# Rotary embedding of split heads: VectorE's program placed at a block of 128 instructions, with landings awaited by other engines

## The chip, the core and the metric

The kernel runs on one core of a Trainium2 chip. The metric is the device time of one execution in microseconds, lower is better. Five engines with instruction streams of their own take part: TensorE (PE), VectorE (DVE), ScalarE (ACT), GpSimd (POOL) and SyncE (SP); 16 DMA engines move data between HBM and the on-chip memory.

## What is computed

`x` has 16 x 512 rows of 1024 floats: 16 heads of 64, each in two halves of 32. `cos` and `sin` have one row of 32 floats for each of the 512 positions. Cut to what matters:

```python
x = x.reshape(batch, seq, num_heads, head_dim)
x1, x2 = x[..., :half_dim], x[..., half_dim:]
rotated = concatenate([x1 * cos - x2 * sin, x1 * sin + x2 * cos], axis=-1)
```

That is 33.55 MB in and 33.55 MB out, in fp32.

## The kernel before

The 8192 rows are cut into 8 tiles of 1024 rows. In a tile each of the 128 partitions holds 8 rows that follow each other in HBM. One such row on all partitions (128 x 1024 floats) is a **unit**; there are 64, and `u` counts them. The tiles lie in a ring of 40 places in `x_sb`, so tiles 5, 6 and 7 reuse the places of tiles 0, 1 and 2 (tile 7 those from 16 on), and a result overwrites its input there.

Each unit takes three steps:

- the **cosine product** x * cos, written to one of three PSUM buffers `t1_ps`: always VectorE, line 347;
- the **sine product** of the swapped halves with (-sin, sin), written to one of six buffers `t2_sb`: GpSimd for most (line 305 two units at once, line 166 one), VectorE for nine (line 166);
- the **sum**: VectorE for 45 units (`comb`, line 356, back into `x_sb`); for the other 19 (`PE2`) TensorE adds `t2_sb` into `t1_ps` through an identity matrix (line 265), and ScalarE copies the result to `x_sb` (line 227).

The order on VectorE is written out: the cosine product of unit `u`, then the sum of unit `u - 1` where that is VectorE's. A cosine product waits until the buffer of unit `u - 3` is free: for a `PE2` unit by ScalarE's semaphore `act`, else by its own semaphore `comb`.

DMA. Nine loads are issued from ScalarE's queue (line 189, q10 in the profile): loads 0 and 1 are the halves of tile 0 (2 MB each), loads 2 to 8 are tiles 1 to 7 (4 MB each). Loads 0 to 5 are issued at once. Loads 6, 7 and 8 (`late`, tiles 5 to 7) are issued in ScalarE's loop behind units 21, 28 and 37, once the stores of the places that they overwrite have landed. The two tables come on the same queue behind load 0 (line 211). Ten stores are issued from SyncE's queue (line 202, q1): two halves of tile 0, tiles 1 to 6, two halves of tile 7. A store waits for the sums of its units, from ScalarE and from VectorE.

Start. VectorE clears a small tile (line 315); TensorE multiplies it six times into `t1_ps` to set PSUM's accumulate bits (line 238, semaphore `sem_w`), and then, once the tables have landed, spreads them into PSUM (line 248). ScalarE makes the sine table from that (lines 222 and 223).

Waits for landings. `wait_landed` waits for `sem_in` of a load at the load's first unit. Before the change GpSimd calls it for each unit (line 291 on) and VectorE does too, in `mul` (line 332). An instruction that needs several semaphores gets a separate semaphore instruction ahead of it, so VectorE's program has 132 instructions: 118 tensor-tensor operations, ten semaphore instructions, one each of drain, memset, scalar product and copy.

Of the kernel before, what the change touches and what calls it, by code (L numbers as in the profile page):

```python
# [6 lines left out]
def bass_split_heads_rope_kernel(  # L7
# [38 lines left out]
    first_row = [sum(t[0] for t in TILES[:i]) for i in range(len(TILES))]  # L46
    NU = sum(t[0] for t in TILES)
    assert NU * P == batch * seq
    NT = len(TILES)
# [3 lines left out]
    loads = []  # L53
# [14 lines left out]
    PE2 = [u in (5, 7) or R1 * 2 <= u < NU - 3 * R1 and u % 8 in (1, 3, 5) for u in range(NU)]  # L68
# [7 lines left out]
    SHARED = 3  # L76
# [4 lines left out]
    NT1 = 3  # L81
    NT2 = 6
    BANK = 512
    EH = H * HD // BANK
    LEAD = 1


    alone = [(not V2[u] or u == SHARED) and not (u and TWO[u - 1]) for u in range(NU)]
# [2 lines left out]
    with ExitStack() as stack:  # L91
# [13 lines left out]
        sem_in = [stack.enter_context(nc.semaphore(f"in{i}")) for i in range(len(loads))]  # L105
# [8 lines left out]
        sem_w = stack.enter_context(nc.semaphore("bits"))  # L114
# [72 lines left out]
        def load(eng, i):  # L187
            t, o, m = loads[i]
            eng.dma_start(in_sbuf(t, o, m), in_dram(xf, t, o, m)).then_inc(sem_in[i], 16)  # L189

        def wait_landed(eng, t, r):
            if (t, r) in load_at:
                eng.wait_ge(sem_in[load_at[t, r]], 16)
# [11 lines left out]
        def on_scalar(ae):  # L205
            early = [i for i in range(len(loads)) if i not in late]
            for i in early:
                load(ae, i)
                if i == 0:
                    for c, (table, sem) in enumerate(((cos, sem_cos), (sin, sem_sin))):  # L210
                        ae.dma_start(stage[:, c, :], table.rearrange("(s r) d -> s (r d)", r=R1)).then_inc(sem, 16)  # L211
            ae.wait_ge(sem_i, 2)
            for n in SIZES:
                m = n // R1
                ae.activation(  # L215
                    pick[n][:],
                    ident[:].rearrange("q (s k) -> q k s", k=m)[:, :, None, :].broadcast_to([P, m, m, P // m]),
                    COPY,
                ).then_inc(sem_g, 1)
            for i, n in enumerate(SIZES):  # L220
                ae.wait_ge(sem_t, i + 1)
                ae.activation(s_sb[n][:, :, 0, :], raw_sin[n], COPY, scale=-1.0)  # L222
                ae.activation(s_sb[n][:, :, 1, :], raw_sin[n], COPY).then_inc(sem_s, 1)  # L223
            for u in range(NU):
                if PE2[u]:
                    ae.wait_ge(sem_e, n_pe[u])
                    ae.activation(xs[:, place_of(u), :], t1_ps[:, u % NT1, :], COPY).then_inc(sem_a, 1)  # L227
                for i in late:
                    if BEHIND[i] == u:
                        for j in TILES[loads[i][0]][4]:  # L230
                            ae.wait_ge(sem_out[j], 16)
                        load(ae, i)

        def on_tensor(pe):
            pe.wait_ge(sem_z, 1)
            for k in range(NT1):
                for b in range(EH):
                    pe.matmul(  # L238
                        t1_ps[:, k, b * BANK:(b + 1) * BANK], zero[:, 0:P], zero[:], start=True, stop=True
                    ).then_inc(sem_w, 1)  # L240
            pe.wait_ge(sem_g, len(SIZES))
            pe.wait_ge(sem_cos, 16)
            pe.wait_ge(sem_sin, 16)
            pe.wait_ge(sem_w, NT1 * EH)
            for n in SIZES:
                for c, to in enumerate((c_ps[n], raw_sin[n])):
                    for k in range(n // R1):
                        ins = pe.matmul(  # L248
                            to[:, k * R1:(k + 1) * R1, :].rearrange("p r d -> p (r d)"),
                            pick[n][:, k].rearrange("q b s -> q (b s)"),  # L250
                            stage[:, c, :],
                            start=c == 0,
                            stop=True,
                            skip_group_check=c == 1,
                        )
                ins.then_inc(sem_t, 1)
            for u in range(NU):
                if not PE2[u]:
                    continue
                if TWO[u - 1]:  # L260
                    pe.wait_ge(sem_q[(u - 1) % NT2], made[u - 1])
                pe.wait_ge(sem_q[u % NT2], made[u])
                t2 = t2_sb[:, u % NT2, :, :, :].rearrange("p h t d -> p (h t d)")
                for b in range(EH):
                    ins = pe.matmul(  # L265
                        t1_ps[:, u % NT1, b * BANK:(b + 1) * BANK],
                        ident[:],
                        t2[:, b * BANK:(b + 1) * BANK],
                        start=False,
                        stop=True,  # L270
                        skip_group_check=True,
                    )
                ins.then_inc(sem_e, 1)

        def on_gpsimd(pl):
            pl.memset(ident[:], 1.0).then_inc(sem_i, 1)  # L276
            pl.wait_ge(sem_i, 1)
            pl.affine_select(  # L278
                out=ident[:],
                in_=ident[:],  # L280
                compare_op=mybir.AluOpType.is_equal,
                fill=0.0,
                base=0,
                pattern=[[-1, P]],
                channel_multiplier=1,
            ).then_inc(sem_i, 1)
            seen = set()
            for u in range(NU):
                t, r = rows[u]
                n = TILES[t][0]  # L290
                wait_landed(pl, t, r)
                if V2[u] and u != SHARED or (u and TWO[u - 1]):
                    continue
                if n not in seen:
                    seen.add(n)
                    pl.wait_ge(sem_s, SIZES.index(n) + 1)
                m = 2 if TWO[u] else 1
                for v in range(u, u + m):
                    if v == u + m - 1 or PE2[v - NT2] != PE2[v + 1 - NT2]:
                        wait_t2_free(pl, v)  # L300
                k = place_of(u)
                if m == 1:
                    heads(pl, u, 0, CUT if u == SHARED else H, s_sb[n][:, r]).then_inc(sem_q[u % NT2], 1)
                else:
                    pl.tensor_tensor(  # L305
                        t2_sb[:, u % NT2:u % NT2 + 2].rearrange("p n h t d -> p (n h) t d"),
                        x_sb[:, k:k + 2, :, ::-1, :].rearrange("p n h t d -> p (n h) t d"),
                        s_sb[n][:, r:r + 2].rearrange("p n t d -> p n (t d)")[:, :, None, :].broadcast_to(
                            [P, 2, H, HD]
                        ),  # L310
                        mult,
                    ).then_inc(sem_q[u % NT2], 1)

        def on_vector(ve):
            ve.memset(zero[:], 0.0).then_inc(sem_z, 1)  # L315
            ve.wait_ge(sem_w, NT1 * EH)
            seen = set()

            def own_sines():
# [8 lines left out]
            def mul(u):  # L328
                t, r = rows[u]
                n = TILES[t][0]  # L330
                k = place_of(u)
                wait_landed(ve, t, r)
                if n not in seen:
                    seen.add(n)
                    ve.wait_ge(sem_t, SIZES.index(n) + 1)
                if u == NT1 - 1:
                    own_sines()
                if V2[u]:
                    wait_t2_free(ve, u)
                    heads(ve, u, CUT if u == SHARED else 0, H, v_ps[n][:, V_ROWS[n].index(r)])  # L340
                if u >= NT1:
                    v = u - NT1
                    if PE2[v]:
                        ve.wait_ge(sem_a, n_pe[v])
                    else:
                        ve.wait_ge(sem_v, n_comb[v])
                ve.tensor_tensor(  # L347
                    t1_ps[:, u % NT1, :].rearrange("p (h d) -> p h d", d=HALF),
                    x_sb[:, k, :, :, :].rearrange("p h t d -> p (h t) d"),
                    c_ps[n][:, r, :][:, None, :].broadcast_to([P, 2 * H, HALF]),  # L350
                    mult,
                ).then_inc(sem_q[u % NT2], 1)
# [9 lines left out]

            for u in range(NU + LEAD):

                ahead = u == SHARED + LEAD
                if ahead:
                    comb(u - LEAD)
                if u < NU:
                    mul(u)
                if u >= LEAD and not ahead and not PE2[u - LEAD]:  # L370
                    comb(u - LEAD)

# [38 lines left out]
```

## Time and profile before

| what | value |
|---|---|
| median of 3 runs | 161.0 us (161.0 to 161.33) |
| the profiled execution | 161.04 us, span 159.8 us |
| VectorE busy | 134.1 us, 84% of the span, 121 instructions |
| GpSimd busy | 126.5 us, 79%, 40 instructions |
| TensorE, ScalarE busy | 56.3 us (35%), 21.8 us (14%) |
| HBM read, written | 33.69 MB, 33.55 MB: 421 GB/s over the span |
| one product or sum on VectorE (128 x 1024) | 1.22 us |
| one double sine product on GpSimd (128 x 2048) | 4.52 us |
| one copy on ScalarE | 1.02 us |

How to read it: the span runs from the first to the last instruction of the profiled execution, and the execution's time has some 1.2 us around it. The page's slices show busy tenths in 40 equal parts of the span. The row DMA is the mean busy share of the 16 DMA engines, and the queue rows give the packets of each queue, their bytes and the time that they took as a share of 16 engines' span. A view of a window counts the packets that start in it. The timeline gives start, length, engine, line, operation, and in brackets the idle time before and what ended it. In the waits, "A <- B" is A's idle time that B ended.

### The profile page before, as it was taken

How to read it: one execution, taken by the hardware profiler on the slowest of the kernel's cores; microseconds unless marked ns; L12 is line 12 of the kernel's file. 1: busy time of each engine (PE TensorE's matmuls, PEld its weight loads, DVE VectorE, ACT ScalarE, POOL GpSimd, SP SyncE). 2: the span in 40 equal slices, each digit the busy share in tenths (PEclk: the TensorE clock that was granted, in tenths of full speed). 3: DMA queues.
4: the chain of work that ended last, by engine and by line, in shares of the span. 5: the costliest groups of instructions: out<-in, count | busy, mean ns of one | idle time of the engine just before them, and what ended most of it. 6: DMA issues, size and time to landing. Idle time of an engine off the chain costs nothing.

```text
span 159.8 us, 449 instructions
## 1 busy us (share of the span) xinstructions
PE 56.3 (35%) x90; PEld 19.6 (12%) x90; DVE 134.1 (84%) x121; ACT 21.8 (14%) x23; POOL 126.5 (79%) x40
## 2 busy tenths in 40 slices
PE   6050007744407740788066407740575000000000
PEld 1040002111102110222021102110220000000000
DVE  0028997999999999998999999999799987999500
ACT  0410000331300330022203300330022000000000
POOL 1009999999999999999999999956999289990000
PEclk9999999999985899557659985899557655555555
DMA  5999998999999999999999999999999999999996
GB/s 172 418 426 459 435 476 336 422 414 418 500 406 455 435 427 394 420 492 402 394 500 410 402 484 427 402 427 484 402 394 509 402 402 476 435 402 443 406 439 287
DMA packets 3025, 67.25 MB, mean 421 GB/s; under 512 B 336, under 2 KB 592, under 8 KB 592
## 3 DMA queue, kind: packets, MB, share of 16 engines
q10 hardware_dynamic: 1584, 33.69, 49.8%
q1 hardware_dynamic: 1440, 33.56, 48.8%
q14 instruction: 1, 0.01, 0.0%
HBM read 33.69 MB, written 33.55 MB: 421 GB/s over the span
## 4 chain that ended last, share of the span: by engine, by line
DMA 45%; DVE 34%; POOL 11%; PE 1%; issue 1%; ACTq 1%; ACT 0%; SPq 0%; POOLq 0%
DMA x_sb<-in_x_dram 21%; DMA out_dram<-x_sb 20%; DVE t_ps L347 18%; DVE x_sb L356 14%; POOL t_sb L305 6%; POOL t_sb L166 5%; DMA stage<-in_sin_dram 4%; DVE t_sb L166 3%; PE tab_ps L248 1%; PE t_ps L248 1%; ACTq L211 0%; ACT sine L222 0%; ACTq L189 0%; ACT sine L223 0%; SPq L177 0%
## 5 line engine op out<-in xcount | busy, mean ns | idle before, releaser
L305 POOL TENSOR_TENSOR t_sb<-x_sb,sine 128x2048 f32<-128x2048 f32 x22 | 99.0, 4524 | 6.6 <-DMA x_sb<-in_x_dram 6.6
L347 DVE TENSOR_TENSOR t_ps<-x_sb,tab_ps 128x1024 f32<-128x1024 f32 x64 | 76.8, 1221 | 11.3 <-PE t_ps L248 9.9
L265 PE MATMUL t_ps<-t_sb,ident 128*128 128x512 f32 x76 | 51.5, 818 | 59.4 <-DVE t_ps L347 38.6
L356 DVE TENSOR_TENSOR x_sb<-t_ps,t_sb 128x1024 f32<-128x1024 f32 x45 | 54.7, 1219 | 3.7 <-POOL t_sb L305 3.0
L166 POOL TENSOR_TENSOR t_sb<-x_sb,sine 128x1024 f32<-128x1024 f32 (+1 forms) x12 | 27.6, 2307 | 10.4 <-ACT sine L223 10.4
L227 ACT ACTIVATE x_sb<-t_ps 128x1024 f32<-128x1024 f32 x19 | 19.4, 1023 | 91.9 <-PE t_ps L265 89.9
L265 PEld LDWEIGHTS t_ps<-t_sb,ident 128*128 128x128 f32 x76 | 17.1, 250 | 92.7 <-issue 53.6
L166 DVE TENSOR_TENSOR t_sb<-x_sb,tab_ps 128x1024 f32<-128x1024 f32 (+1 forms) x9 | 10.1, 1124 | 0.0
L238 PE MATMUL t_ps<-zero 128*128 128x512 bf16 x6 | 2.7, 630 | 1.3 <-DVE zero L315 1.3
L248 PE MATMUL tab_ps<-stage,chosen 128*128 128x128 f32 x4 | 1.2, 454 | 4.9 <-DMA stage<-in_sin_dram 4.9
L215 ACT ACT_TABLE_LOAD x1 | 1.3, 1283 | 4.8 <-issue 4.8
L248 PEld LDWEIGHTS tab_ps<-stage,chosen 128*128 128x128 f32 x4 | 0.9, 322 | 5.8 <-issue 5.8
L248 PE MATMUL t_ps<-stage,chosen 128*128 128x128 f32 x4 | 1.1, 421 | 0.0
L315 DVE MEMSET zero<- 128x256 uint32 x1 | 0.3, 272 | 0.9 <-PEq L393 0.9
L238 PEld LDWEIGHTS t_ps<-zero 128*128 128x128 bf16 x6 | 0.7, 137 | 2.4 <-DVE zero L315 1.2
L222 ACT ACTIVATE sine<-t_ps 128x256 f32<-128x256 f32 x1 | 0.4, 383 | 4.4 <-PE t_ps L248 4.4
L248 PEld LDWEIGHTS t_ps<-stage,chosen 128*128 128x128 f32 x4 | 1.0, 333 | 0.0
L276 POOL MEMSET ident<- 128x128 f32 x1 | 0.2, 204 | 0.3 <-POOLq L393 0.3
L215 ACT ACTIVATE chosen<-ident 128x256 f32<-128x256 f32 x1 | 0.4, 429 | 0.0
L223 ACT ACTIVATE sine<-t_ps 128x256 f32<-128x256 f32 x1 | 0.4, 378 | 0.0
L278 POOL TENSOR_SCALAR_AFFINE_SELECT ident<-ident 128x128 f32<-128x128 f32 x1 | 0.3, 292 | 0.1
L393 POOL MEMSET const-float32-0.0<- 128x1 f32 x1 | 0.1, 98 | 0.3 <-issue 0.3
(5 smaller groups left out, 0.7 us busy)
## 6 DMA issues: line engine op xcount, KB each, us to landing
x_sb<-in_x_dram ACTq DMA_DIRECT2D x7, 4096.0 KB, 33.2
out_dram<-x_sb SPq DMA_DIRECT2D x6, 4096.0 KB, 30.2
out_dram<-x_sb SPq DMA_DIRECT2D x4, 2048.0 KB, 16.4
x_sb<-in_x_dram ACTq DMA_DIRECT2D x2, 2048.0 KB, 9.4
stage<-in_cos_dram ACTq DMA_DIRECT2D x1, 64.0 KB, 7.2
stage<-in_sin_dram ACTq DMA_DIRECT2D x1, 64.0 KB, 7.0
```

The lines of the kernel that those rows point to most:

```text
L166: return eng.tensor_tensor(t2_sb[:, u % NT2, a:b, :, :], swapped(place_of(u))[:, a:b], table[:, None, :, :].broadcast_to([P, b - a, 2, HALF]),
L215: ae.activation(pick[n][:], ident[:].rearrange("q (s k) -> q k s", k=m)[:, :, None, :].broadcast_to([P, m, m, P // m]), COPY,).then_inc(se ...
L222: ae.activation(s_sb[n][:, :, 0, :], raw_sin[n], COPY, scale=-1.0)
L223: ae.activation(s_sb[n][:, :, 1, :], raw_sin[n], COPY).then_inc(sem_s, 1)
L227: ae.activation(xs[:, place_of(u), :], t1_ps[:, u % NT1, :], COPY).then_inc(sem_a, 1)
L238: pe.matmul(t1_ps[:, k, b * BANK:(b + 1) * BANK], zero[:, 0:P], zero[:], start=True, stop=True).then_inc(sem_w, 1)
L248: ins = pe.matmul(to[:, k * R1:(k + 1) * R1, :].rearrange("p r d -> p (r d)"), pick[n][:, k].rearrange("q b s -> q (b s)"), stage[:, c, :] ...
L265: ins = pe.matmul(t1_ps[:, u % NT1, b * BANK:(b + 1) * BANK], ident[:], t2[:, b * BANK:(b + 1) * BANK], start=False, stop=True, skip_group ...
L278: pl.affine_select(out=ident[:], in_=ident[:], compare_op=mybir.AluOpType.is_equal, fill=0.0, base=0, pattern=[[-1, P]], channel_multiplier=1,
L305: pl.tensor_tensor(t2_sb[:, u % NT2:u % NT2 + 2].rearrange("p n h t d -> p (n h) t d"), x_sb[:, k:k + 2, :, ::-1, :].rearrange("p n h t d ...
L347: ve.tensor_tensor(t1_ps[:, u % NT1, :].rearrange("p (h d) -> p h d", d=HALF), x_sb[:, k, :, :, :].rearrange("p h t d -> p (h t) d"), c_ps ...
L356: ve.tensor_tensor(xs[:, place_of(u), :], t1_ps[:, u % NT1, :], t2_sb[:, u % NT2, :, :, :].rearrange("p h t d -> p (h t d)"), add,).then_i ...
```

## The change

Four edits move VectorE's waits for landings to other engines, and one places its program.

- VectorE's wait for the six zero products (`sem_w`) goes; TensorE itself waits for them before the tables, as before.
- VectorE waits for a landing only in the last tile (`in8`). For the rest:
  - TensorE waits for load 0 before it spreads the tables, which VectorE waits for;
  - GpSimd waits for load 1 before the sine product of unit 3 (`SHARED`), whose sum comes before VectorE's first product of load 1;
  - ScalarE waits for the load of tiles 1 to 6 before its copy of the unit three ahead of the tile's first (units 5, 13, 21, 29, 37 and 45, the `carrier`s), since VectorE's first product of the tile waits for that copy.
- `addr_align(128, offset=0, max_nops=0)` behind VectorE's memset asks the loader to put the next instruction at a multiple of 128 places in VectorE's stream; the padding is jumped over.

VectorE's program has 125 instructions afterwards, the directive among them, and 121 behind the directive. The order of the arithmetic and of the DMAs on each engine is unchanged; ScalarE has six more semaphore instructions.

```diff
+    BLOCK = 128
...
+        carrier = {}
+        for i, (t, o, _) in enumerate(loads):
+            if t == 0:
+                assert o in (0, SHARED + 1)
+            elif t < NT - 1:
+                assert PE2[first_row[t] - NT1]
+                carrier[first_row[t] - NT1] = i
...
                 if PE2[u]:
+                    if u in carrier:
+                        ae.wait_ge(sem_in[carrier[u]], 16)
                     ae.wait_ge(sem_e, n_pe[u])
...
             pe.wait_ge(sem_w, NT1 * EH)
+            pe.wait_ge(sem_in[0], 16)
...
                 wait_landed(pl, t, r)
+                if u == SHARED:
+                    wait_landed(pl, t, r + 1)
...
             ve.memset(zero[:], 0.0).then_inc(sem_z, 1)
-            ve.wait_ge(sem_w, NT1 * EH)
+
+            ve.addr_align(BLOCK, offset=0, max_nops=0)
...
-                wait_landed(ve, t, r)
+                if t == NT - 1:
+                    wait_landed(ve, t, r)
```

## Prediction

> **What bounds the kernel.** I read the page's slices and its DMA queues first, since VectorE is 84% busy but the busiest row of all is the DMA's:
>
> ```profile
> DMA  5999998999999999999999999999999999999996
> ...
> q10 hardware_dynamic: 1584, 33.69, 49.8%
> q1 hardware_dynamic: 1440, 33.56, 48.8%
> q14 instruction: 1, 0.01, 0.0%
> ```
>
> Loads (q10) and stores (q1) take 49.8% + 48.8% = 98.6% of what 16 DMA engines have in the span; only the first and the last slice are open. The packet records behind this row agree: 1,664 packets of 32 KB at 1.213 us and 768 of 16 KB at 0.611 us are 2,487 us, or 155.5 us on each of 16 engines, and each engine starts between 1.82 and 2.87 us and is then never free until it ends. So a shorter wait on VectorE moves nothing as long as the DMA queues hold work, and the time is that of the DMA engine that ends last.
>
> The third queue is the one that the change is about: one packet of instructions inside the span. A window of 10 ns finds it, and the timeline of VectorE shows what ran:
>
> ```profile
> DMA packets 1, 0.01 MB, mean 819 GB/s; under 512 B 0, under 2 KB 0, under 8 KB 0
> ...
> q14 instruction: 1, 0.01, 193.1%
> ```
>
> ```profile
> 63.49 1.22 DVE L347 TENSOR_TENSOR t_ps<-x_sb,tab_ps 128x1024 f32<-128x1024 f32 x1
> 64.62 1.22 DVE L356 TENSOR_TENSOR x_sb<-t_ps,t_sb 128x1024 f32<-128x1024 f32 x1
> 65.75 1.22 DVE L347 TENSOR_TENSOR t_ps<-x_sb,tab_ps 128x1024 f32<-128x1024 f32 x1
> 66.88 1.21 DVE L166 TENSOR_TENSOR t_sb<-x_sb,tab_ps 128x1024 f32<-128x1024 f32 x1
> ```
>
> The packet starts at 65.52 us, has 8,192 bytes and takes 0.309 us. VectorE starts an instruction every 1.13 us straight across it: the fetch did not hold VectorE. Whose fetch is it? If a packet is a block of 128 instructions, as the change takes it, VectorE's 132 can't lie in one block and must enter another once; the span has one such packet, and VectorE runs about its 56th instruction. The other candidate is PE, with 90 weight loads and 90 matmuls in the trace, which started again at 64.86 us after 6 us of idle time. I take it to be VectorE's, by the count, and keep PE for a rival.
>
> What the fetch does hold is the DMA engine that carried it. In the packet records that engine's next packet (32 KB, at 65.82) takes 1.564 us for 1.213; with the fetch it lost 0.309 + 0.351 = 0.66 us. Every transfer closes with a 4-byte packet on each of the 16 engines (under 512 B in the rows). Load 5 closes first 15 times by 69.38 us, then once at 69.81; the final store closes 15 times by 159.03 and once at 159.41. Three windows, 69.4 to 69.9, 158.6 to 159.03 and 159.03 to 159.8:
>
> ```profile
> DMA packets 3, 0.07 MB, mean 131 GB/s; under 512 B 1, under 2 KB 1, under 8 KB 1
> ```
> ```profile
> DMA packets 16, 0.02 MB, mean 38 GB/s; under 512 B 15, under 2 KB 15, under 8 KB 15
> ```
> ```profile
> DMA packets 1, 0.00 MB, mean 0 GB/s; under 512 B 1, under 2 KB 1, under 8 KB 1
> ```
>
> The reader is to see one straggler, alone, from the fetch to the end of the span. Packet by packet, end to start, the chain from the fetch leads to load 5's straggler. At load 4's close, before the fetch, the last two engines are 0.04 us apart (51.19 and 51.23), not 0.43.
>
> **The change part by part.** All sums are against the profiled execution, 161.04 us with its span of 159.8 (1.24 lie around it); the median of the runs is 161.0, so I forecast on 161.04 and compare with 161.0.
>
> 1. *The alignment.* The directive becomes padding that is jumped over once, behind the memset at 0.92 us. VectorE then waits for the tables until 11.09 (9.9 us idle, released by PE L248), which hides a jump of any price below that. Behind it stand 121 instructions, so 7 places of 128 are left and the program crosses no block between 11 and 150 us. The fetch at 65.5 goes. Without its 0.66 us the straggler would end at 158.75, and the 15 others set the end. What is late next is the second engine: 0.38 us earlier by packets (159.41 to 159.03), or 0.27 us by the semaphore's steps (159.76 to 159.49), since landings are reported at different delays. The gain is 0.27 to 0.38.
>
> [...] No row shows a fetch during the start. Bounds: 0 (before the first load packet at 1.82) and 0.66 us of straggling as at 65.5. I take 0 to 0.3: engines whose first packets come 1.05 us apart (1.82 to 2.87) close load 0 within 0.46 us (7.75 to 8.21 by the semaphore's steps), so a late starter catches up more than half. That leaves at most 158.75 + 0.3 = 159.05, level with the second engine, and costs nothing.
>
> [...]
>
> 2. *VectorE's waits.* Of ten semaphore instructions eight go, with the waits for eight landings and for the zeros of PE. They last 0.02 to 0.05 us and lie beside the running operation (starts stay 1.13 us apart across them): worth 0. PE's added wait for load 0 (landed 8.21 us) stands before the wait for the tables' data (8.65): 0. GpSimd's added wait for load 1 (landed 13.49) stands before its fourth product, at about 18 us: 0.
>
> 3. *ScalarE's six added waits.* Behind each stands a copy (L227) and whatever VectorE and the stores wait for of it. Landings against the copy's start: load 2 at 23.2 against 28.9, load 3 at 37.0 against 43.1, load 4 at 51.6 against 58.9, load 5 at 70.3 against 76.2, load 6 at 89.6 against 91.1: five come earlier and cost 0. Load 7 comes at 109.00, its copy was at 106.94:
>
> ```profile
> 106.94 1.02 ACT L227 ACTIVATE x_sb<-t_ps 128x1024 f32<-128x1024 f32 x1 [2.43 <-PE t_ps L265]
> 109.24 1.22 DVE L347 TENSOR_TENSOR t_ps<-x_sb,tab_ps 128x1024 f32<-128x1024 f32 x1
> 111.66 0.33 SPq L202 DMA_DIRECT2D out_dram<-x_sb  x1
> 113.61 1.23 DVE L356 TENSOR_TENSOR x_sb<-t_ps,t_sb 128x1024 f32<-128x1024 f32 x1 [0.89 <-POOL t_sb L305]
> ```
>
> That copy moves to about 109.0 and ends at 110.0; VectorE's product at 109.24 needs it and moves to about 110.1, 0.85 late. Two more operations follow, then the 0.89 us in which VectorE waits for GpSimd takes it up: back in step at 113.6. The store at 111.66 leaves at about 112.5; the store before it lands at 130.8, so the queue is covered for 18 us. Load 8 was issued earlier, at 95.2. Cost 0.
>
> Sum: 161.04 − 0.27 to 0.38 = 160.66 to 160.77. I forecast **160.7 us**.
>
> **Rivals.**
>
> *Nothing gained, 161.0.* The fetch stays under the loads or stores once and the straggler remains: because the jump's fetch costs its whole 0.66 at the start, because seven instructions beyond the last one enter the next block at 150 us, because the fetch was PE's, or because the padding is not placed as the directive asks (the change would then not do what it says). Against: the count above, and the catching up in the first 6 us. For: PE's start at 64.86, 0.66 us ahead of the packet, and no row tells what VectorE executes after 150 us.
>
> [...]
>
> *Two fetches instead of one, slower: 161.3 to 161.7.* The block is entered at 1 us, and, since only 7 places are left behind the 121, the next one at about 150 us, when VectorE is done and stores still run until 159.4. Should both fall on the same DMA engine under traffic, it loses 1.32 us for 0.66: at most 161.04 + 0.66 = 161.70; with half of the first caught up 161.04 + 0.3 = 161.34. It decides only if VectorE passes those 7 places before 159 us.
>
> *ScalarE's late copy starves the stores, 161.2 to 161.9.* VectorE's 0.85 us at 109 would have to reach the end, in part or whole (161.04 + 0.85 = 161.89). The last store is issued at 150.09, and the one ahead of it closes at 154.55, so 4.4 us are covered; for a loss of even 0.2 us the delay must grow past 4.6. I see no such growth.
>
> **How the numbers follow.** Forecast 0.60, no gain 0.25, two fetches 0.10, late copy 0.05. A measurement of this kernel tells about 0.2%, 0.32 us, from no change. The forecast's gain lies just around that: 0.27 and 0.38 on one side and the other, up to 0.66 if the straggler also held back others. Of its 0.60 I put 0.41 beyond 0.2% and 0.19 within. Faster 0.41; within 0.19 + 0.25 = 0.44; slower 0.10 + 0.05 = 0.15. The range: 161.04 − 0.66 = 160.4 below; above, no gain with the spread of the runs (161.33) and the cheap end of the two fetches (161.34): 161.4. It leaves out some 0.15.
>
> **What would show it.** Right: queue q14 has no packet between 5 and 159 us, at most one near 1 to 3; the last window holds no lone 4-byte packet 0.4 us behind the rest; 14 of 16 engines close load 5 within about 0.3 us (two come earlier, as before); VectorE's row at 109 is about 0.85 late, and in step again at 113.6. Wrong: a q14 packet at 150 us or midway, a straggler with no fetch in the span, or a DMA slice below 9 between the first and the last.

## The result, and the profile after

The changed kernel takes 162.39 us (median of 6 runs, 161.93 to 162.54) for 161.0 before: a ratio of 1.0079, with a 95% interval of 1.0068 to 1.009. It is slower by 0.8%; the forecast was 160.7, in a range of 160.4 to 161.4.

The profiled execution takes 161.93 us with a span of 160.07; before it was 161.04 with 159.79. So of 0.89 us more in the profiles, 0.28 lie in the span and 0.61 around it (1.86 for 1.25). Over all six runs the time around the span is 1.83 to 2.04, and the span 160.0 to 160.5, in four of them 160.5.

The page's DMA rows, for those of before: full to the same extent, and again one packet of instructions in the span.

```profile
DMA  5999998999999999999999999999999999999896
...
q10 hardware_dynamic: 1584, 33.69, 49.7%
q1 hardware_dynamic: 1440, 33.56, 48.7%
q14 instruction: 1, 0.01, 0.0%
```

But the packet has moved. The window from 4.68 to 4.70 us holds it, and the one from 161.5 to 162.5 us, behind the span, a second one:

```profile
DMA packets 1, 0.01 MB, mean 410 GB/s; under 512 B 0, under 2 KB 0, under 8 KB 0
...
q14 instruction: 1, 0.01, 98.8%
```
```profile
DMA packets 1, 0.01 MB, mean 8 GB/s; under 512 B 0, under 2 KB 0, under 8 KB 0
...
q14 instruction: 1, 0.01, 2.1%
```

The straggler is there from the start. Load 0 lands on 15 DMA engines by 8.15 us and on the last at 9.12 (before: 8.18 and 8.21). The window from 8.3 to 9.3 us has three late closing packets, the last ones of load 0 and of the two tables; before (the first line) it has none:

```profile
DMA packets 27, 0.44 MB, mean 442 GB/s; under 512 B 0, under 2 KB 0, under 8 KB 0
```
```profile
DMA packets 48, 0.48 MB, mean 483 GB/s; under 512 B 3, under 2 KB 19, under 8 KB 19
```

At the end the windows 158.5 to 159.2 and 159.2 to 159.8 us show it as before, 15 closing packets and then a single one; the packet records put them at 159.07 and 159.70 (before 159.03 and 159.41):

```profile
DMA packets 16, 0.02 MB, mean 23 GB/s; under 512 B 15, under 2 KB 15, under 8 KB 15
```
```profile
DMA packets 1, 0.00 MB, mean 0 GB/s; under 512 B 1, under 2 KB 1, under 8 KB 1
```

The timeline around 109 us shows ScalarE's copy waiting for load 7, as the prediction had it, and VectorE back near its old place (113.98 for 113.61):

```profile
109.19 1.02 ACT L241 ACTIVATE x_sb<-t_ps 128x1024 f32<-128x1024 f32 x1 [3.33 <-DMA x_sb<-in_x_dram]
109.46 1.21 DVE L375 TENSOR_TENSOR x_sb<-t_ps,t_sb 128x1024 f32<-128x1024 f32 x1
110.59 1.22 DVE L366 TENSOR_TENSOR t_ps<-x_sb,tab_ps 128x1024 f32<-128x1024 f32 x1
...
113.01 0.33 SPq L214 DMA_DIRECT2D out_dram<-x_sb  x1
113.98 1.21 DVE L375 TENSOR_TENSOR x_sb<-t_ps,t_sb 128x1024 f32<-128x1024 f32 x1
```

### The profile page after: what moved, and what is told of

It reads as the page before. It is cut to its first block, busy times and chain, and to the rows that moved or that the text cites. A ratio compares the mean times of both kernels' runs of the same rounds, so it can differ in the third digit from the quotient of the medians.

```text
span 160.1 us, 448 instructions
## 1 busy us (share of the span) xinstructions
PE 56.6 (35%) x90; PEld 19.9 (12%) x90; DVE 134.0 (84%) x121; ACT 21.8 (14%) x23; POOL 126.5 (79%) x40
## 4 chain that ended last, share of the span: by engine, by line
DMA 45%; DVE 35%; POOL 11%; PE 1%; ACTq 1%; ACT 0%; issue 0%; SPq 0%; POOLq 0%
DMA x_sb<-in_x_dram 21%; DMA out_dram<-x_sb 19%; DVE t_ps L366 18%; DVE x_sb L375 14%; POOL t_sb L322 6%; POOL t_sb L167 5%; DMA stage<-in_sin_dram 5%; DVE t_sb L167 3%; PE tab_ps L263 1%; PE t_ps L263 1%; ACTq L223 0%; ACT sine L234 0%; ACTq L190 0%; ACT sine L235 0%; SPq L178 0%
```

## The experiments

Two theories stood against each other. **Placement**: the fetch at 4.69 us makes a worse straggler than the one at 65.5, and VectorE's end, 7 places ahead of a block's end, costs time behind the span. **Waits**: the moved waits cost the time. Each diff is against the changed kernel unless it says otherwise. "Lag" is the last DMA engine's closing packet of the final store less the last but one, in the profiled execution (a second late engine makes it small: in e1 the last three close at 159.03, 159.30 and 159.43); "around" is the time less the span, over all runs of the kernel. "Left" is the number of places from the program's end to the next multiple of 128, as the directive sets it.

| kernel | left | fetches, us | lag, us | profiled span, us | around, us | median, us | ratio to before (95%) |
|---|---|---|---|---|---|---|---|
| before | | 65.52 | 0.38 | 159.8 | 1.2 to 1.3 | 161.0 | |
| changed | 7 | 4.69, 161.89 | 0.63 | 160.1 | 1.83 to 2.04 | 162.39 | 1.0079 (1.0068 to 1.009) |
| e1 waits only | | 64.32 | 0.13 | 159.8 | 1.19 to 1.29 | 161.1 | 1.0005 (0.9996 to 1.0014) |
| e2 align only | 127 | 3.77, 133.95 | 2.31 | 161.7 | 1.21 to 1.28 | 162.37 | 1.009 (1.0069 to 1.0112) |
| e3 offset 64 | 71 | 4.58, 68.92 | 1.63 | 161.0 | 1.20 to 1.30 | 161.88 | 1.0051 (1.0032 to 1.0071) |
| e4 offset 112 | 23 | 5.68 | 1.34 | 160.8 | 1.19 to 1.27 | 161.7 | 1.0045 (1.0031 to 1.006) |
| e5 offset 7 | 0 | 4.45, 133.36 | 1.69 | 161.1 | 1.19 to 1.28 | 162.31 | 1.0068 (1.0049 to 1.0087) |
| e6 offset 124 | 11 | 5.74 | 0.95 | 160.4 | 1.20 to 1.29 | 161.77 | 1.0039 (1.0025 to 1.0054) |
| e7 offset 98 | 37 | 30.16 | 0.14 | 159.6 | 1.19 to 1.29 | 160.89 | 0.9988 (0.9978 to 0.9998) |
| e8 padding run through | 7 | 7.46, 161.95 | 0.78 | 160.2 | 1.79 to 1.96 | 162.28 | 1.0066 (1.0048 to 1.0085) |
| e9 offset 127 | 8 | 5.25, 162.29 | 0.98 | 160.5 | 2.04 | 162.34 | 1.0083 (1.0064 to 1.0102) |
| e10 offset 4 | 3 | 4.66, 161.82 | 0.80 | 160.5 | 1.36 to 1.58 | 162.01 | 1.006 (1.0037 to 1.0083) |
| e11 offset 104 | 31 | 20.10 | 0.62 | 160.4 | 1.20 to 1.28 | 161.41 | 1.0025 (1.0015 to 1.0035) |
| e12 offset 98 again | 37 | 30.46 | 0.49 | 159.9 | 1.20 to 1.29 | 160.92 | 0.9997 (0.9988 to 1.0006) |

**The halves apart: e1 and e2.** e1 leaves the directive out:

```diff
-            ve.addr_align(BLOCK, offset=0, max_nops=0)
```

> The changed kernel without the alignment directive: VectorE's waits are moved, its program lies where it lay. Two theories. Placement: the loss of the changed kernel comes from the placement alone, in two pieces. The fetch at 4.69 us makes one DMA engine close everything 0.6 to 1.0 us after the others (span 160.07 for 159.79 in the profiles, 160.5 in most timed runs), and VectorE's program, ending 7 places before a block's end, crosses into the next block after the span (161.93 - 160.07 = 1.86 us around the span for 161.04 - 159.79 = 1.25). Then this kernel takes 161.0 us, with 1.2 to 1.3 us around the span, no fetch before 60 us and one at 65 to 73 us (eight semaphore instructions less, so the block's end falls some five operations of 1.13 us later). Waits: the loss comes from the moved waits (tables 0.8 us later, ScalarE's copy held for load 7). Then it takes 162.2 to 162.5 us. If the fetch stays at 65.5 us, it is not VectorE's place that sets it.

161.1 us, the same as before, and 1.2 us around the span. The moved waits cost nothing that can be measured: the theory of the waits falls. One detail was expected wrongly: the fetch came at 64.32 us and not some five operations later. VectorE had 75 instructions left there, the running one among them, and 76 in the kernel before. Eight instructions fewer moved the block's end with the program's end, as if a program without the directive were laid by its end.

e2 is the kernel before with the directive alone:

```diff
             ve.memset(zero[:], 0.0).then_inc(sem_z, 1)
+            ve.addr_align(128, offset=0, max_nops=0)
```

> The kernel before with the alignment directive behind VectorE's memset and nothing else: 129 instructions stand behind the directive, one more than 128. Placement: one fetch at about 4.7 us as in the changed kernel and a second one when the last instruction is reached, at 147 to 151 us, under the stores. The straggler then loses some 0.66 us more: span 160.7 to 161.2; the program ends one place into a fresh block, so 1.2 to 1.3 us around the span; in all 162.0 to 162.4. Waits: no wait is moved, so 161.0 us.

162.37 us, from the directive alone: placement. Both fetches are there and the time around the span is 1.21 to 1.28, but the second came at 133.95 us, when VectorE was 15 instructions ahead of the multiple, and not at 147 to 151. The straggler closed 2.31 us behind the others, more than the two fetches account for: it was 0.96 us behind at load 0 and 1.70 at load 8, still ahead of the second fetch. That the time is so near the changed kernel's 162.39 is chance, since all of e2's loss lies in the span and half of the changed kernel's around it.

**Other places in the block: e3 and e4.** One number is changed:

```diff
-            ve.addr_align(BLOCK, offset=0, max_nops=0)
+            ve.addr_align(BLOCK, offset=64, max_nops=0)   # e4: offset=112
```

> The changed kernel with the program placed 64 places behind a multiple of 128. It enters a block by the jump and crosses the next multiple after 64 instructions, and ends 57 places into that block, with 71 left. Placement: two fetches, at about 4.7 us and at 70 to 80 us, both under traffic; span 160.7 to 161.2 us; 1.2 to 1.3 us around the span since no end of a block is near; in all 162.0 to 162.4. If instead the jump itself costs the time around the span, 1.86 us stay around it and the whole is 162.6 to 163.0. Waits: 162.2 to 162.5 with nothing changed against the changed kernel.

> The changed kernel with the program placed 112 places behind a multiple of 128. The program before crossed its block's end at about its 54th instruction, so it lies some 76 places into a block at the directive; place 112 is then in the same block, and no block is entered at the start. [...] Placement: no fetch at 4.7 us, one at 20 to 26 us; load 0 closes on all engines by 8.3 us; the straggler loses 0.66 us or less, since packets are slow from 24 to 35 us anyway (0.65 us a DMA engine in the profile of before), so the span is 159.4 to 159.8; the crossing behind the span stays, 1.86 us around it; in all 161.3 to 161.7. If the jump costs the time around the span and not the crossing: 161.3 to 161.7 too, but then offset 64 keeps 1.86. Waits: 162.2 to 162.5.

e3 had its two fetches (4.58 and 68.92 us) and 1.25 us around the span, so the jump by itself does not cost the time there; 161.88 us is a little less than expected. e4 gave 161.7 us as a number, but neither way of getting it held: the fetch was at the start (5.68 us) although no block should have been entered, and the time around was 1.19 to 1.27 us, not 1.86. That 23 places left cost time behind the span was an estimate: no row shows how many instructions VectorE runs there. No other fetch follows in e4. The window 5.67 to 5.70 us has the fetch, and in the packet records the engine's next packet, 16 KB, takes 1.147 us for 0.611: with the fetch 0.85 us lost. (The changed kernel's fetch lost about as much: 0.316 us, and 1.134 for 0.611 in the packet behind it.) At the end (159.1 to 160.7 us) one engine still moves two data packets when the rest has closed:

```profile
DMA packets 2, 0.02 MB, mean 819 GB/s; under 512 B 0, under 2 KB 0, under 8 KB 0
...
q10 hardware_dynamic: 1, 0.02, 127.3%
q14 instruction: 1, 0.01, 64.4%
```
```profile
DMA packets 3, 0.03 MB, mean 20 GB/s; under 512 B 1, under 2 KB 1, under 8 KB 1
```

So 161.7 - 161.0 = 0.7 us of the loss belong to a fetch at the start and what becomes of it (the engine was 0.76 us behind at load 0 and 1.34 at the end), and the rest of the changed kernel's 1.39 us, 0.7, is what it has more around the span. The changed kernel's own runs divide the same way: the median span is 160.5 us, for 159.7 in the runs of before beside e1, and some 1.9 us lie around it for 1.24.

**What costs behind the span: e5, e6, e8, e9, e10.** e5 is `offset=7`, e6 `offset=124`, e9 `offset=127`, e10 `offset=4`; e8 runs through the padding:

```diff
-            ve.addr_align(BLOCK, offset=0, max_nops=0)
+            ve.addr_align(BLOCK, offset=0, max_nops=255)
```

> The changed kernel with the program 7 places behind a multiple of 128, so that its last instruction is the last place of its block. In the runs so far a fetch came when VectorE was 14 to 15 instructions ahead of a multiple (offset 64: the 50th behind the directive; alignment alone: the 113th), and only the changed kernel, which ends 7 places ahead of one, has 1.83 to 2.04 us around the span; all others have 1.2 to 1.3. If what follows the kernel pays for the crossing, this kernel, where nothing but what follows lies behind the multiple, shows whether it is the crossing itself or the few places left: with 1.2 to 1.3 around the span the few places are what costs, with 1.8 to 2.0 any end up to the multiple does. If the fetch comes 14 to 15 instructions ahead whatever the program does, there are two: at 4 to 6 us and at about 141 us, and the span is 161.0 to 161.7, in all 162.2 to 163. If there is no second fetch, the span is 160.0 to 160.5 and the whole 161.3 to 162.5.

> The changed kernel with the program 124 places behind a multiple of 128: it crosses after 4 instructions and ends 11 places ahead of the next multiple. If few places left behind the program cost the time around the span, by the distance of 14 to 15 instructions seen at the other fetches, 1.8 to 2.0 us stand around the span (23 left at offset 112: 1.2 to 1.3). If it is the placement at a multiple itself, 1.2 to 1.3. One fetch at 4 to 6 us, the straggler as at offset 112, span 160.2 to 160.8. In all 162.0 to 162.8 by the first, 161.4 to 162.1 by the second.

> The changed kernel with max_nops=255: VectorE runs through the padding instead of jumping over it; the program lies at the same multiple of 128 and ends 7 places ahead of the next. If the jump makes the fetch late and dear, the fetch comes earlier or as it came before, close to the first packets at 1.8 to 3 us, and the straggler loses less: span 159.5 to 159.8. If only the place counts, the fetch stays at 4 to 6 us with a span of 160.0 to 160.5. Around the span 1.8 to 2.0 us in both, since the end lies where it lay; with 1.2 to 1.3 there the jump would be the cause.

> The changed kernel with the program 127 places behind a multiple of 128: it ends 8 places ahead of one (the changed kernel: 7, with 1.79 to 2.04 us around the span whether the padding is jumped over or run through; offset 124: 11, with 1.20 to 1.29). If the places left at the end decide, the turn lies between 7 and 11 and this run places it: 1.8 to 2.0 or 1.2 to 1.3. If it is the program's first place, exactly a multiple, that costs, 1.2 to 1.3 here and in the next run. One fetch at 4 to 6 us, span 160.2 to 160.8.

> The changed kernel with the program 4 places behind a multiple of 128, ending 3 places ahead of the next. Offset 7, ending at the multiple, had a second fetch at 133.4 us, 16 instructions ahead of its end; the changed kernel, ending 7 ahead, had none before its end and one at 161.9 us, behind the span. If VectorE reads its program some 16 places ahead but not past the end of the kernel's part, this run has no second fetch under the stores, 1.8 to 2.0 us around the span and 162.0 to 162.5 in all. If it reads on past the end by a few places, there is a second fetch at 133 to 142 us, a span of 161.0 to 161.7 and 1.2 to 1.3 around it: again 162.2 to 162.9.

e5 ends at the multiple and has 1.19 to 1.28 us around; its second fetch came at 133.36 us, 16 instructions ahead of the end, under the stores, and not at 141. e6 with 11 left has 1.20 to 1.29: the distance of 14 to 15 does not decide there. e8 has 1.79 to 1.96 with no jump, so the jump is not the cause; nor is the early fetch, which e3 to e6 have too. e9 with 8 left has 2.04, so the turn lies between 8 and 11. Its first place is not a multiple, while e2 starts at one, ends elsewhere and has 1.21 to 1.28: it is the end that counts. e10 with 3 left has 1.36 to 1.58, neither of the two that were expected. In all four with 3 to 8 left, and in no other, a fetch is seen behind the span. The window 161 to 163 us of e9 and the same of e4 (23 left):

```profile
DMA packets 1, 0.01 MB, mean 4 GB/s; under 512 B 0, under 2 KB 0, under 8 KB 0
...
q14 instruction: 1, 0.01, 1.7%
```
```profile
DMA packets 0, 0.00 MB, mean 0 GB/s; under 512 B 0, under 2 KB 0, under 8 KB 0
```

So the four programs that end 3, 7 or 8 places ahead of a multiple of 128 paid some 0.1 to 0.8 us behind the span. The packet records tie this to the fetch seen there, counted from the span's start:

| kernel | fetch starts, us | takes, us | ends, us | execution, us | difference, us |
|---|---|---|---|---|---|
| changed | 161.886 | 0.342 | 162.23 | 161.93 | 0.30 |
| e8 | 161.948 | 0.342 | 162.29 | 161.99 | 0.30 |
| e9 | 162.294 | 0.549 | 162.84 | 162.54 | 0.30 |
| e10 | 161.818 | 0.493 | 162.31 | 162.01 | 0.30 |

The difference is that of the fetch's end and the execution's time. It is the same in all four, while the fetch's start lies 0.04 to 0.25 us ahead of that time: the execution's end follows the fetch's end. (If it waits for the fetch, the execution's time is counted from at least 0.3 us behind the span's start; no row shows where the count begins.) Why 11 places left are free, what asks for a fetch 1.3 to 1.8 us behind the span, and why VectorE, 7 or 11 places ahead, does not fetch before its end as it does at 0, stays open.

**Where a fetch costs least: e7, e11 and e12.** `offset=98` (e7, e12) and `offset=104` (e11) put the fetch into the stretch of slow packets at 24 to 35 us (0.65 us a DMA engine over 1.213 and 0.611 a packet in the profile of before), and ahead of it:

> The changed kernel with the program 98 places behind a multiple of 128: the multiple lies 30 instructions ahead, so by the distance of 14 to 15 the fetch comes at the 15th or 16th instruction behind the directive, 25 to 29 us, and none at the start; 37 places are left at the end, so 1.2 to 1.3 us around the span. From 24 to 35 us the packets of all 16 DMA engines are slow (0.5 to 0.65 us an engine in all). If an engine that loses time there catches up, the straggler is gone: span 159.4 to 159.6, in all 160.6 to 160.9, below both kernels. If it doesn't, it loses 0.66 us as at 65 us: 161.0 to 161.1, the same as before.

> The changed kernel with the program 104 places behind a multiple of 128: the multiple lies 24 instructions ahead, so the fetch comes 13 to 16 ahead of it, at the 8th to 11th instruction, 17 to 23 us, while only loads run. With offset 98 the fetch came at 30.2 us, in the stretch of slow packets, and the last DMA engine ended 0.14 us behind the others (0.38 in the kernel before). If slow packets that follow let the engine catch up, the same here: span 159.5 to 159.7, 160.7 to 160.9 in all. If only a fetch within that stretch is free, the engine stays 0.4 to 0.7 behind: span 159.7 to 160.1, 161.0 to 161.4.

> Offset 98 once more with more rounds, since its first ratio of 0.9988 had an interval of 0.9978 to 0.9998: if it is faster than the kernel before, the interval stays below 1 at 0.998 to 0.9995, with 160.8 to 160.95 us; if that was chance, 161.0 and an interval that holds 1.

e7 was at 0.9988 with the interval just below 1, e12 with more runs at 0.9997 (0.9988 to 1.0006): no gain that is shown over the kernel before. It does beat the changed kernel, by 1.5 us. The fetch itself was not free: in e12 it takes 0.309 us at 30.46, and the 16 KB packet behind it 0.956 for 0.611, 0.65 us lost as in the middle of the kernel before. e11, with the fetch at 20.10 us, lost 0.98 us (0.320, and 1.875 for 1.213), closed load 3 0.96 us behind the others and the final store 0.62, and took 161.41: with the slow packets behind it the engine caught up a part at most.

## Why the prediction was wrong, point by point

- *What bounds the kernel.* Right. In each of the traces the span ends some 0.4 us behind one DMA engine's last closing packet (159.79 and 159.41 before, 160.07 and 159.70 changed) and moves with it: the kernel before with one fetch and e2, which adds the directive alone, with two, differ by 1.4 us, with the same arithmetic.
- *Whose fetch it is.* Right: it moved with VectorE's place in every run, while PE's program is the same in the changed kernel and in e1 and e3 to e12. That VectorE was entering the block was not quite right: the fetch comes 13 to 16 instructions ahead of the multiple (e2, e3, e5, e7, e11). The early fetches fit this too. e8 runs through 60 padding instructions, so the directive stands at place 68 of a block: offsets 0 to 64 lie in the next block, and e3 fetched soon after its jump; offsets 98 to 127 lie in the same one, and e4, e6 and e9 (16, 4 and 1 places ahead of the multiple) fetched while VectorE waited for the tables (5.25 to 5.74 us), e7 and e11 (30 and 24) only later (30.16 and 20.10). Which instructions a packet brings no row shows.
- *The 0.66 us of the fetch at 65.5.* Right in size: by the packet records 0.65 to 0.66 us again at 64, 69, 134 and 30 us.
- *The fetch at the start costs nothing.* **This step failed.** The fetch at 65.5 did go. That another comes at the start was my estimate, and the changed kernel shows it. For it I took 0 to 0.3 us, from engines that start 1.05 us apart and close load 0 within 0.46. The fetch did not come near the first load packet, but at 4.69 us, 3.8 us after the jump at 0.86, and the engine then closed load 0 0.97 us behind the others and the final store still 0.63 behind. Why engines that start late catch up and this one did not is open. The upper bound, 0.66, was itself too low for a fetch while only loads run: 0.84 here, 0.85 in e4, 0.98 at 20 us in e11. The late engine gave a span of 160.0 to 160.5 us in place of 159.4 to 159.5. The rival of no gain had this cost among its reasons, at 0.66.
- *The time around the span.* **This term was missing.** I carried 1.24 us over from the kernel before, and used the 7 places left only for a crossing under the stores at 150 us. VectorE did not cross there. The program's end so near a multiple cost 0.6 to 0.8 us behind the span, where no rival looked: a fetch from 161.89 to 162.23 us, whose end the execution's end follows.
- *ScalarE's copy at 109.0.* Right (109.19, released by load 7), and even cheaper than thought: VectorE was 1.36 us behind already (107.20 for 105.84) and did not wait for the copy at all.
- *VectorE's, PE's and GpSimd's waits cost 0.* Right by e1, in the time: its VectorE ran up to 1.26 us later in between (109.37 for 108.10) and ended 0.20 ahead (149.82 for 150.02). In the changed kernel the tables come later (VectorE's first product at 11.83 for 11.09), since the straggler carries a part of the tables too (the sine table lands at 9.54 for 8.65). That is no wait of the change; the delay reached the last operation of VectorE with 0.17 us (150.19 for 150.02), with a queue of stores ahead.
- *Two fetches* was the rival on the right side, with a straggler of more than one loss, but its place was wrong: its second fetch at 150 us did not happen in the changed kernel. e2 and e5 are that rival, with the second fetch at 133 to 134 us, and at 162.3 to 162.4 us they lie beyond its bound of 161.7.
- *A block of 128 instructions.* It was taken from the change, and the runs fit it: e5, which starts 7 places behind a multiple of 128 and ends at the next, has two fetches (4.45 us, and 133.36 with 8,192 bytes). VectorE itself isn't held (before, it starts an instruction every 1.13 us across the fetch at 65.52), but where a fetch falls under traffic shows in the time: e11 and e12, with one each at 20.10 and 30.46 us, take 161.41 and 160.92.

## What to carry to other kernels

Where the DMA engines are full from first to last, look at the last engine's closing packets: here one packet of 8 KB on one of 16 engines, an instruction fetch, set the end (0.66 us lost at 65.5 us, the last closing packet 0.38 us behind the others). Moving it did not remove it (at 4.69 us it lost 0.84, and the last closing packet was 0.63 behind); ask where a fetch lands, and price it by a run at that place, not by a fetch elsewhere. And compare the time around the span too, and look for a fetch behind the span, since the changed kernel's end cost 0.6 to 0.8 us there, which no engine's row shows.

## What was not expected of the hardware

- An 8 KB fetch cost its DMA engine two to three times its own 0.31 us, because the next packet took 0.34 to 0.66 us longer (1.564 for 1.213 us at 65 us, 1.875 for 1.213 at 20).
- VectorE's fetch came 13 to 16 instructions ahead of a multiple of 128 (e2, e3, e5, e7, e11), counted where its packet starts. At the start the packet came late: 2.9 to 3.8 us after the jump at 0.86 us (changed kernel, e2, e3, e5, e10), and in e8, which runs through its padding until 3.65, at 7.46.
- The programs that end 3, 7 or 8 places ahead of such a multiple have 1.36 to 2.04 us around the span, for 1.2 to 1.3 at 0, 11, 23, 31, 37, 71 and 127 places.
- A straggler can grow without another fetch: in e4 it landed load 5 0.85 us behind the others (70.54 and 69.69), load 8 1.44 behind (129.21 and 127.77); in the changed kernel it shrank from 0.97 at load 0 to 0.63 at the end. Why is open.
